# A two-layer decoder trunk on one core: the instruction planner's count of needed buffers, its look-ahead limits, the order of the mixers' steps, and an early preparation of one weight block

## The chip, the core and the metric

The program runs on 1 core of one Trainium2 chip. The metric is the device time of one execution in microseconds (us). One execution of the kernel before was recorded by the hardware profiler, and all rows in this text come from that recording. The engines are named as the profile names them: PE multiplies matrices, PEld loads its weights, DVE (VectorE) and ACT (ScalarE) work element by element, POOL is GpSimd, and SP only issues transfers.

## What is computed

A sequence of 512 positions with 1024 features goes through two layers. Each layer adds three normalized branches to x:

```python
for i in range(DEPTH):                       # DEPTH = 2
    h = rmsnorm(x, mix_pre_g[i])
    z = h @ w_in[i]                          # split into the inputs of three mixers
    out_a = spatial_gating(...)              # 4 groups of 64, chunks of 128 positions
    out_b = silu(r_g) * rms(retention(...))  # 6 heads of 64, a state carried over 4 chunks
    out_c = forgetting_attention(...)        # 6 heads of 64, softmax with decay
    x = x + rmsnorm(concat(out_a, out_b, out_c) @ w_o[i], mix_post_g[i])
    h = rmsnorm(x, ffn_pre_g[i])
    f = (gelu(causal_conv3(h @ w_gate[i])) * (h @ w_up[i])) @ w_down[i]   # width 4096
    x = x + rmsnorm(f, ffn_post_g[i])
    gate = sigmoid(rmsnorm(x, ple_pre_g[i]) @ w_ple_gate[i])
    x = x + rmsnorm((p[i] @ w_ple_proj[i]) * gate, ple_post_g[i])
```

## The kernel before

Products of full precision are made of three faster ones: `split` writes a high part (a cast on ACT) and a low part (a subtraction on DVE) of each operand, and `mm3` issues three matmuls (high with high, high with low, low with high). The positions are four chunks c of 128 (`NCH`), the 1024 features eight blocks of 128 (`KB`).

A layer is recorded by four functions in turn. `mixers` runs a list of steps: u and s the gating, F and v values of attention and retention, g0 to g2 and L the retention's gate (L is its Silu), f, a the projections and the softmax of a pair of attention heads, r, c those of a pair of retention heads. Each writes blocks of the concatenated result `cc`. `out_proj` multiplies `cc` by w_o: the first 512 columns (banks `wo0`) feature block by feature block in `O_ORDER` as the blocks of `cc` come, then the other 512 chunk by chunk. When a chunk is complete, `post_chunk` makes the row sums, the normalized branch (`fo`) and the new x, and `nxt` makes h, whose transposes (`hps`) PE computes. `ffn` works through 32 blocks b of 128 features. For the gate and up projections each block uses seven products instead of eight (12 matmuls of 128x256 each): the class `Seven` makes the seven sums of h that stand on their left (`hb..`, `hh..`, `hd`), and `gate_up` the sums of the weights that stand on their right. A block's weights come as `graw` (two transfers of 512 KB); from it come `wg` (split of the raw weights), `wu`, then four additions in place on `graw`, then `wsa` and `wsb` (splits of the sums). PE accumulates b11 and h6 in `beta`, b21 and d in `ag`, and ACT copies `beta` to `gs` after each of b11 and h6; the product h6 (`beta<-hh,wsa`) adds to the same place, so it follows the first copy. `down` multiplies the activations of four blocks by w_down (`dn`). `embed_operands` and the `eps` matmuls make p @ w_ple_proj for `ple`. All transfers are issued on SP's one queue.

Nothing of this is issued where it is written. A class `Plan` records every operation, and at the end `issue` simulates the engines with a cost for each operation and fixes the order of every engine's instructions; the chip then runs each engine's list in that order, with waits between engines. An operation whose inputs are ready is taken when it also has its buffers. The limits are:

- `AHEAD`: a buffer is not taken if its first use lies more than so many operations ahead of the oldest unfinished one; there is a number for each stage (`gu0` for the first four blocks of `ffn`, `gu` for the others, `emb`, `wo2` and so on).
- `live[tag]` counts, for every operation of the written order, how many buffers of a kind are needed there; a buffer is taken ahead of its turn only where that leaves enough. `inside[c]` is the same count for the two sets of 8 KB buffers (`SETS`: X has 18, W has 6; `wg`, `wsa` and `wsb` live only in W).

`SWITCH` is what the planner charges PE for going from one kind of matmul to another, and `warm` (in the changed code) stands for PE's full clock. All operations are issued from one line, L444 (L448 in the changed code), so the tile's name tells what an instruction is.

Of the kernel before, what the change touches and what calls it, by code (L numbers as in the profile page):

```python
# [50 lines left out]
class Plan:  # L51
# [153 lines left out]
    def cost(self, engine, method, outs, ins, args, kw):  # L205
# [13 lines left out]
        if engine == "PE":  # L219
            if method == "transpose":  # L220
                return 108, 0, n, "T"
            dt, rows = kw["lhsT"].dtype, kw["lhsT"].shape[0] / P
            if dt == F32R:
                return 0.4427 * n, 0, n * rows, n
            half = 0.5 if kw["lhsT"].shape[0] == 64 or kw["lhsT"].shape[-1] == 64 else 1
            return half * max(222, n * 4 / 2.4 + 4), 0, 2 * n * rows, "F"
        if engine == "ACT":
# [19 lines left out]
    def issue(self):  # L247
        ops = self.ops
        n = len(ops)
# [33 lines left out]
        order = []  # L283
        then, kind = None, "T"
        parked = {tag: [] for tag in (*slots, *(f"b8 {k}" for k in (*self.SETS, None)))}
# [65 lines left out]
        def complete(i, now):  # L351
            nonlocal front
            freed = []
            for t in set(ops[i][5]):
                uses[t] -= 1
                if not uses[t]:
                    tag = self.tiles[t][0]
                    heapq.heappush(slots[tag], now)
                    if t in self.kind:
                        c, k = self.place[t]  # L360
                        heapq.heappush(unused[c], (now, k))
                        freed += [f"b8 {k}" for k in (*self.SETS, None)]
                    freed.append(tag)
# [24 lines left out]
        while len(order) < n:  # L388
            progress = False
            for e in names:  # L390
# [3 lines left out]
                if ready[e] and free[e] <= now:  # L394
# [7 lines left out]
                    if e == "PE":  # L402
                        then = self.follows.get(i)
                        if ops[i][6][3] != kind:
                            busy += self.SWITCH.get(kind, 0) + (95 if ops[i][6][3] == "F" else 25 if ops[i][6][3] == 512 else 0)
# [112 lines left out]
def body(ctx, tc, a, out):  # L518
# [299 lines left out]

    def mixers(l, hT, uv):
        rs = hT.rs  # L820
# [243 lines left out]
        fq, rq = {}, {}  # L1064
        for step in "u F s g1 f0 g0 v a0 f1 a1 g2 r0 f2 L c0 r1 a2 r2 c1 c2".split():
            h = int(step[1]) if len(step) > 1 else 0
# [14 lines left out]
            elif step == "L":  # L1081
                A.activation(sg, sg, AF.Silu)
            elif step[0] == "f":
                fq[h] = fox_proj(h)
# [9 lines left out]

    def out_proj(l, cc, x, new, g, nxt):

# [20 lines left out]
        tm_chunk_major(cc, u, 512, done, O_ORDER, (0, 2, 1, 3))  # L1117
        return emb

    def ffn(l, hs, emb, x, new, g, nxt):  # L1120
        h = hs.t
# [15 lines left out]
        def gate_up(b, between):  # L1137
            raw = b8("graw", (2048,))
            load(raw, a["w_gu"][l, b].rearrange("p s n -> p (s n)"))
            u2, u1, g1, g2 = (raw[:, i * 512:i * 512 + 512] for i in range(4))  # L1140
            wg = b8("wg", (2, 1024), F32R)
            split(wg[:, 0, :], wg[:, 1, :], raw[:, 1024:2048])
            wu = [wk("wu", dt=F32R) for _ in range(2)]
            split(wu[0], wu[1], u2)
            for t, by in ((g1, u1), (u1, u2), (u2, g1), (g2, u2)):
                V.tensor_tensor(out=t, in0=t, in1=by, op=ALU.add)
            sa = b8("wsa", (2, 1024), F32R)
            split(sa[:, 0, :], sa[:, 1, :], raw[:, 0:1024])
            sb = b8("wsb", (2, 1024), F32R)
            split(sb[:, 0, :], sb[:, 1, :], raw[:, 1024:2048])  # L1150

            beta, ag = bank("beta"), bank("ag")
# [202 lines left out]
    for l in range(DEPTH):  # L1355
        cc = mixers(l, hT, uv)
        g = Gains(("mix_post_g", l), ("ffn_pre_g", l))
        hs = Seven(g)
        emb = out_proj(l, cc, Rows(src), xd[3 * l], g, hs)
        g = Gains(("ffn_post_g", l), ("ple_pre_g", l))  # L1360
        hT = Plain(g)
        ffn(l, hs, emb, Rows(xd[3 * l]), xd[3 * l + 1], g, hT)
        last = l + 1 == DEPTH
# [32 lines left out]
```

## Time and profile before

| | |
|---|---|
| median of 3 executions | 1589.41 us (1588.22 to 1592.01) |
| profiled execution | 1587.76 us, of it 1585.7 us in the span of the core |
| PE busy | 1559.8 us, 98% of the span |
| DVE busy | 1233.2 us, 78% |
| ACT busy | 837.2 us, 53% |
| POOL busy | 91.3 us, 6% |
| mean granted PE clock | 0.996 of full speed |

The span is the stretch from the first to the last instruction; the execution's own time holds 2.1 us more. Busy times of different engines overlap. In rows of instructions the columns are the start in us, the duration, engine and line, operation, output and inputs by the names in the program (buffer numbers left out), the tile's size, and how many instructions were joined; in brackets stands how long the engine stood idle before and which instruction of which engine ended that.

### The profile page before, as it was taken

The numbers are of one execution on the slowest core, as the hardware profiler recorded it, in microseconds if no ns is written. First come the engines' busy times: TensorE is split into PE (matmuls) and PEld (weight loads), VectorE is DVE, ScalarE is ACT, GpSimd is POOL, SyncE is SP. The second block draws the span as 40 slices with busy tenths as digits, with TensorE's granted clock in tenths as the row PEclk, the third lists the DMA queues.
The fourth block names the chain that finished last, engine by engine and source line by source line (L and its number), as shares of the span: only waits on it lengthen the run. The fifth ranks groups of instructions, "written<-read, shape, count | busy, mean of one in ns | idle before, by whom it ended". The sixth has DMA issues, their size and how long they took to land.

```text
span 1585.7 us, 25202 instructions
## 1 busy us (share of the span) xinstructions
PE 1559.8 (98%) x10034; PEld 1388.1 (88%) x10034; DVE 1233.2 (78%) x2013; ACT 837.2 (53%) x1380; POOL 91.3 (6%) x157
## 2 busy tenths in 40 slices
PE   7999998999999999999999999989999999999998
PEld 6887787999999999998888777889999999999987
DVE  6556869988878888878664658699887897898785
ACT  7324637665555555554552446477655555555453
POOL 1100020000000000002220000200000000000021
PEclk9999999999999999999999999999999999999999
DMA  8113147223323422424463023362332233234433
GB/s 316 68 55 107 61 168 265 81 80 115 125 81 103 137 80 88 153 100 180 179 250 107 28 80 116 125 252 81 108 116 97 92 123 106 83 131 134 148 141 124
DMA packets 63421, 197.47 MB, mean 125 GB/s; under 512 B 7348, under 2 KB 15164, under 8 KB 63304
## 3 DMA queue, kind: packets, MB, share of 16 engines
q1 hardware_dynamic: 63160, 195.81, 35.1%
q8 instruction: 78, 1.28, 0.3%
q14 instruction: 39, 0.32, 0.1%
q10 hardware_dynamic: 144, 0.07, 0.0%
HBM read 178.52 MB, written 17.33 MB: 124 GB/s over the span
## 4 chain that ended last, share of the span: by engine, by line
PE 95%; DVE 2%; DMA 1%; ACT 1%; POOL 0%; issue 0%; SPq 0%; POOLq 0%; DVEq 0%; ACTq 0%
PE beta L444 22%; PE dn L444 22%; PE ag L444 16%; PE ps L444 15%; PE rps L444 4%; PE fps L444 4%; PE gps L444 2%; PE wo L444 2%; PE sps L444 1%; PE hps L444 1%; PE tps L444 1%; PE ops L444 1%; PE rops L444 1%; DMA graw<-in_w_gu_dram 1%; PE ips L444 0%
## 5 line engine op out<-in xcount | busy, mean ns | idle before, releaser
L444 PE MATMUL dn<-thl,act 128*128 128x512 f32 x1536 | 371.4, 391 | 0.0
L444 PEld LDWEIGHTS dn<-thl,act 128*128 128x128 f32 x1536 | 279.9, 188 | 51.9
L444 PE MATMUL ps<-thl,hT 128*128 128x512 f32 (+3 forms) x984 | 207.1, 368 | 0.1
L444 PEld LDWEIGHTS ps<-thl,hT 128*128 128x128 f32 x984 | 177.0, 189 | 23.3 <-DVE thl L444 1.2
L444 DVE TENSOR_TENSOR graw<-graw 128x512 f32<-128x512 f32 x256 | 169.2, 684 | 1.0
L444 DVE TENSOR_TENSOR thl<-traw,thl 128x1024 fp32r<-128x1024 f32 (+2 forms) x120 | 140.4, 1184 | 13.6 <-ACT thl L444 13.6
L444 ACT CAST thl<-traw 128x1024 fp32r<-128x1024 f32 (+2 forms) x120 | 120.1, 1018 | 9.0 <-DMA traw<-in_w_pg_dram 4.6
L444 PE MATMUL beta<-hh,wsa 128*128 128x256 f32 x768 | 101.4, 281 | 7.8 <-ACT gs L444 7.5
L444 PEld LDWEIGHTS beta<-hh,wsa 128*128 128x128 f32 x768 | 94.7, 192 | 8.7 <-ACT gs L444 7.9
L444 PEld LDWEIGHTS beta<-hb,wg 128*128 128x128 f32 x768 | 97.7, 189 | 4.9
L444 PEld LDWEIGHTS beta<-hh,wu 128*128 128x128 f32 x768 | 98.2, 189 | 4.2
L444 PE MATMUL beta<-hh,wu 128*128 128x256 f32 x768 | 100.4, 280 | 0.0
L444 PE MATMUL beta<-hb,wg 128*128 128x256 f32 x768 | 99.9, 278 | 0.0
L444 PE MATMUL ag<-hb,wg 128*128 128x256 f32 x768 | 98.6, 276 | 0.0
L444 PE MATMUL ag<-hd,wsa 128*128 128x256 f32 x768 | 98.5, 278 | 0.0
L444 PE MATMUL beta<-hh,wsb 128*128 128x256 f32 x768 | 98.4, 276 | 0.0
L444 DVE SCALAR_TENSOR_TENSOR cv<-gs,cw,cv 128x511 f32<-128x511 f32 (+1 forms) x128 | 95.1, 743 | 3.6 <-ACT cv L444 3.5
L444 PE MATMUL ag<-hb,wsb 128*128 128x256 f32 x768 | 97.9, 276 | 0.0
L444 ACT ACTIVATE cv<-gs,cw 128x512 f32<-128x512 f32 x64 | 52.2, 816 | 82.4 <-DVE gs L444 82.4
L444 ACT COPY gs<-beta 128x256 f32<-128x256 f32 x128 | 47.2, 371 | 88.4 <-PE beta L444 86.6
L444 DVE TENSOR_TENSOR wsb<-graw,wsb 128x1024 fp32r<-128x1024 f32 x64 | 78.0, 1219 | 19.8 <-ACT wsb L444 15.0
L444 PEld LDWEIGHTS ag<-hd,wsa 128*128 128x128 f32 x768 | 93.1, 190 | 0.0
(193 smaller groups left out, 2655.7 us busy)
## 6 DMA issues: line engine op xcount, KB each, us to landing
graw<-in_w_gu_dram SPq DMA_DIRECT2D x128, 512.0 KB, 6.2
traw<-in_w_dn_dram SPq DMA_DIRECT2D x64, 512.0 KB, 5.0
x<-x SPq DMA_DIRECT2D x40, 512.0 KB, 5.0
fraw<-in_w_fm_dram SPq DMA_DIRECT2D x30, 512.0 KB, 8.8
traw<-in_w_wo_dram SPq DMA_DIRECT2D x16, 512.0 KB, 4.2
traw<-in_w_pg_dram SPq DMA_DIRECT2D x16, 512.0 KB, 8.6
x<-in_x_dram SPq DMA_DIRECT2D x8, 512.0 KB
traw<-in_w_uv_dram SPq DMA_DIRECT2D x8, 512.0 KB, 8.1
```

Of the source, the lines that this page charges most:

```text
L444: made = o[1](*[self.map(v) for v in o[2]], **{k: self.map(v) for k, v in o[3].items()})
```

## The change

Four edits stand beside each other. (1) When the last user of a buffer completes, `issue` now lowers `live` and `inside` from the oldest unfinished operation up to that buffer's last use, so that buffers that were taken and returned ahead of their turn are no longer counted as needed. (2) `AHEAD`, `SWITCH` and the clock's model have other numbers, and matmuls of 64 rows or columns are a kind of their own. (3) The mixers' steps and the last two of `O_ORDER` stand in another order. (4) The weight work of a block is a function of its own, `gate_up_weights`, and for block 0 it is recorded in `out_proj` after the first completed chunk (`EARLY`), in place of `gate_up`. The chip's instructions are the same in number and shape, but for ACT's table loads, 15 in place of 17.

```diff
-    AHEAD = {"mix": 460, "wo": 230, "wo2": 230, "emb": 185, "gu0": 720, "gu": 460, "dn": 245, "end": 770, "pg": 450, "pg2": 120}
+    AHEAD = {"mix": 595, "wo": 404, "wo2": 214, "emb": 291, "gu0": 1206, "gu": 523, "dn": 1028, "end": 1710, "pg": 555, "pg2": 142}
-    SWITCH = {"F": 110, "T": 9}
+    SWITCH = {"F": 40, "H": 310, "T": 9}
...
                     heapq.heappush(slots[tag], now)
+                    live[tag][front:last[t] + 1] -= 1
                     if t in self.kind:
                         c, k = self.place[t]
+                        inside[c][front:last[t] + 1] -= 1
                         heapq.heappush(unused[c], (now, k))
...
-                        if columns.get(now // self.TICK - 1, 0) < self.WARM:
+                        if not warm:
                             busy *= 2
-                        tick = (now + busy) // self.TICK
-                        columns[tick] = columns.get(tick, 0) + ops[i][6][2]
+                            tick = (now + busy) // self.TICK
+                            columns[tick] = columns.get(tick, 0) + ops[i][6][2]
+                            warm = columns.get(now // self.TICK - 1, 0) >= self.WARM
...
-O_ORDER = (0, 1, 5, 6, 7, 2, 3, 4)
+STEPS = "u g1 F g0 f0 s v f1 a0 g2 L a1 f2 r0 r1 a2 c0 r2 c2 c1"
+O_CHUNKS = (0, 2, 1, 3)
+EARLY = {0: 0}
+O_ORDER = (0, 1, 5, 6, 7, 2, 4, 3)
...
-        for step in "u F s g1 f0 g0 v a0 f1 a1 g2 r0 f2 L c0 r1 a2 r2 c1 c2".split():
+        for step in STEPS.split():
...
+    def gate_up_weights(l, b):
+
+        stage, plan.stage = plan.stage, "gu0" if b < 4 else "gu"
+        raw = b8("graw", (2048,))
+        load(raw, a["w_gu"][l, b].rearrange("p s n -> p (s n)"))
+        u2, u1, g1, g2 = (raw[:, i * 512:i * 512 + 512] for i in range(4))
+        wg = b8("wg", (2, 1024), F32R)
+        split(wg[:, 0, :], wg[:, 1, :], raw[:, 1024:2048])
+        wu = [wk("wu", dt=F32R) for _ in range(2)]
+        split(wu[0], wu[1], u2)
+        for t, by in ((g1, u1), (u1, u2), (u2, g1), (g2, u2)):
+            V.tensor_tensor(out=t, in0=t, in1=by, op=ALU.add)
+        sa = b8("wsa", (2, 1024), F32R)
+        split(sa[:, 0, :], sa[:, 1, :], raw[:, 0:1024])
+        sb = b8("wsb", (2, 1024), F32R)
+        split(sb[:, 0, :], sb[:, 1, :], raw[:, 1024:2048])
+        plan.stage = stage
+        return wg, wu, sa, sb
...
+            if len(seen) in EARLY:
+                ready[EARLY[len(seen)]] = gate_up_weights(l, EARLY[len(seen)])
+            seen.append(c)
...
+            wg, wu, sa, sb = gate_up_weights(l, b) if b not in ready else ready[b]
```

What this does to the issued order is seen in rows of the two orders. The first place is DVE at the entry of layer 0's `ffn`. Numbers tell tiles apart: before, `graw_1969` holds block 0's weights, and `graw_2352` those of block 1.

```order
L444 TENSOR_TENSOR graw_1969<-graw_1969 128x512
L444 TENSOR_TENSOR wg_2420<-graw_2352,wg_2420 128x1024
L444 TENSOR_TENSOR hh4_2290<-s4_2425,hh4_2290 128x4x128
L444 TENSOR_TENSOR graw_1969<-graw_1969 128x512
L444 TENSOR_TENSOR wu_2444<-graw_2352,wu_2414 128x512
L444 TENSOR_TENSOR graw_1969<-graw_1969 128x512
L444 TENSOR_TENSOR graw_2352<-graw_2352 128x512
L444 TENSOR_TENSOR graw_1969<-graw_1969 128x512
L444 TENSOR_TENSOR graw_2352<-graw_2352 128x512
L444 TENSOR_TENSOR wsa_2459<-graw_1969,wsa_2459 128x1024
L444 TENSOR_TENSOR gs_2474<-ag_2469,gs_2474 128x256
```
In the changed order block 0's weights are `graw_1913`, and its additions stand in `out_proj`, among the first chunks' `fo` and x.

```order
L448 TENSOR_TENSOR graw_1913<-graw_1913 128x512
L448 TENSOR_TENSOR fo_2092<-wo0_1713,gain_1903 128x512
L448 TENSOR_TENSOR fo_2092<-wo0_1761,gain_1903 128x512
L448 TENSOR_TENSOR graw_1913<-graw_1913 128x512
L448 TENSOR_TENSOR fo_2106<-wo0_1768,gain_1903 128x512
L448 TENSOR_TENSOR fo_2106<-wo0_1809,gain_1903 128x512
L448 TENSOR_TENSOR fo_2092<-ps_2049,gain_1903 128x512
L448 TENSOR_TENSOR graw_1913<-graw_1913 128x512
L448 SCALAR_TENSOR_TENSOR x_1874<-fo_2092,y_2113,x_1874 128x1024
L448 TENSOR_TENSOR graw_1913<-graw_1913 128x512
L448 TENSOR_TENSOR wsa_2130<-graw_1913,wsa_2130 128x1024
```
All four additions and `wsa` of block 0 stand now ahead of every h of `out_proj`. Before, they stood behind the last of the seven sums of h, alternating with the same work for block 1.

The second place is ACT just ahead of the first copy of `beta` to `gs`, before the change.

```order
L444 CAST hh7_2266<-s7_2400 128x4x128
L444 CAST hh6_2258<-s6_2405 128x4x128
L444 CAST wu_2414<-graw_2352 128x512
L444 COPY e_2322<-eps_2396 128x512
L444 CAST wg_2420<-graw_2352 128x1024
L444 CAST hh4_2290<-s4_2425 128x4x128
L444 COPY e_2354<-eps_2422 128x512
L444 CAST wu_2437<-graw_2375 128x512
L444 COPY e_2354<-eps_2440 128x512
L444 CAST wsa_2459<-graw_1969 128x1024
L444 COPY gs_2474<-beta_2450 128x256
```
The cast of `wsa` for block 0 stands directly ahead of the copy. In the changed order there are two pieces; in the first, the casts of block 0's `wu`, `wg` and `wsa` stand behind `pT`, the transposed p of `embed_operands`.

```order
L448 CAST pT_2051<-pps_2041 128x256
L448 CAST pT_2051<-pps_2046 128x256
L448 CAST wu_2060<-graw_1913 128x512
L448 CAST wg_2068<-graw_1913 128x1024
L448 CAST pT_2051<-pps_2063 128x256
L448 ACTIVATE junk_100,s1_2102<-ps_2049 128x512
L448 CAST wsa_2130<-graw_1913 128x1024
```
The second piece is the one that ends in the same copy.

```order
L448 CAST wg_2403<-graw_2258 128x1024
L448 COPY e_2312<-eps_2381 128x512
L448 CAST wg_2421<-graw_2275 128x1024
L448 COPY s22_2433<-hps_2419 128x512
L448 COPY e_2383<-eps_2401 128x512
L448 CAST hd_2266<-sd_2430 128x4x128
L448 CAST hb22_2288<-s22_2433 128x4x128
L448 CAST hh6_2282<-s6_2442 128x4x128
L448 COPY e_2383<-eps_2428 128x512
L448 CAST hh7_2273<-s7_2460 128x4x128
L448 COPY gs_2482<-beta_2445 128x256
```
In place of the cast of block 0's `wsa` there stand two `wg` of the blocks 1 and 2 (`graw_2258`, `graw_2275`), farther ahead. On SP the loads of the blocks 1 to 3 follow those of x in one piece now, ahead of the first stores of e.

The third place is PE from the transposes of the first chunks' h up to h6 of block 0, before the change.

```order
L444 MATMUL hps<-k_ident,h 128x128 x4
L444 MATMUL eps<-ehl,pT 128x512 x3
L444 MATMUL hps<-k_ident,h 128x128 x4
L444 MATMUL eps<-ehl,pT 128x512 x18
L444 MATMUL hps<-k_ident,h 128x128 x8
L444 MATMUL eps<-ehl,pT 128x512 x18
L444 MATMUL beta<-hb_2163,wg 128x256 x12
L444 MATMUL ag<-hb_2175,wg 128x256 x12
L444 MATMUL beta<-hh_2258,wsa 128x256 x2
L444 MATMUL beta<-hb_2163,wg 128x256 x5
L444 MATMUL beta<-hh_2258,wsa 128x256 x10
```
In the changed order the same stretch reads as follows.

```order
L448 MATMUL hps<-k_ident,h 128x128 x4
L448 MATMUL eps<-ehl,pT 128x512
L448 MATMUL hps<-k_ident,h 128x128 x4
L448 MATMUL eps<-ehl,pT 128x512 x24
L448 MATMUL hps<-k_ident,h 128x128 x4
L448 MATMUL eps<-ehl,pT 128x512
L448 MATMUL hps<-k_ident,h 128x128 x4
L448 MATMUL eps<-ehl,pT 128x512 x7
L448 MATMUL beta<-hb_2179,wg 128x256 x12
L448 MATMUL ag<-hb_2191,wg 128x256 x12
L448 MATMUL beta<-hb_2179,wg 128x256 x3
L448 MATMUL beta<-hh_2282,wsa 128x256 x12
```
More `eps` stand between the second and the third group of transposes, fewer behind the fourth, and three matmuls of block 1 stand ahead of h6 (`beta<-hh_2282,wsa`).

## Rows read from the trace of the kernel before

**Rows 1.** The page: busy time by engine, and the chain that ended last.

```profile
PE 1559.8 (98%) x10034; PEld 1388.1 (88%) x10034; DVE 1233.2 (78%) x2013; ACT 837.2 (53%) x1380; POOL 91.3 (6%) x157
...
PE 95%; DVE 2%; DMA 1%; ACT 1%; POOL 0%; issue 0%; SPq 0%; POOLq 0%; DVEq 0%; ACTq 0%
```
**Rows 2.** Waits of PE: for what, us in total, times, longest us.

```profile
PE hps L444 <- DVE h L444: 7.9, 1, 7.9
PE beta L444 <- ACT gs L444: 7.5, 2, 3.8
PE hps L444 <- ACT wg L444: 1.8, 2, 0.9
PE cps L444 <- DVE ro L444: 1.2, 2, 0.7
PE beta L444 <- DVE wsa L444: 0.3, 1, 0.3
```
**Rows 3.** Timeline of PE, entry of layer 0's `ffn`.

```profile
254.72 4.36 PE L444 MATMUL eps<-ehl,pT 128*128 128x512 f32 x18
...
260.33 1.58 PE L444 MATMUL ag<-hb,wg 128*128 128x256 f32 x12
265.68 0.51 PE L444 MATMUL beta<-hh,wsa 128*128 128x256 f32 x2 [3.77 <-ACT gs L444]
```
**Rows 4.** Timeline of PE, the same place in layer 1.

```profile
1049.28 0.80 PE L444 MATMUL beta<-hh,wsa 128*128 128x256 f32 x2 [3.75 <-ACT gs L444]
```
**Rows 5.** Timeline of ACT, the same place in layer 0.

```profile
264.31 1.04 ACT L444 CAST wsa<-graw 128x1024 fp32r<-128x1024 f32 x1 [1.71 <-DVE graw L444]
265.26 0.36 ACT L444 COPY gs<-beta 128x256 f32<-128x256 f32 x1
```
**Rows 6.** Timeline of DVE, the same place in layer 0.

```profile
252.77 1.41 DVE L444 SCALAR_TENSOR_TENSOR h<-x,rs,gain 128x512 f32<-128x512 f32 x2 [1.44 <-POOL rs L444]
...
263.59 2.49 DVE L444 TENSOR_TENSOR graw<-graw 128x512 f32<-128x512 f32 x4
266.00 1.22 DVE L444 TENSOR_TENSOR wsa<-graw,wsa 128x1024 fp32r<-128x1024 f32 x1
```
**Rows 7.** Timeline of SP, block 1's weights in layer 0.

```profile
251.44 1.43 SPq L444 DMA_DIRECT2D graw<-in_w_gu_dram  x2
```
**Rows 8.** Windows: length, busy us of PE, PEld, DVE, ACT, POOL, PE clock, DMA share, GB/s.

```profile
220.00:240.00 20.00, 20.00 (x98) 16.49 (x97) 13.78 (x22) 10.54 (x27) 4.84 (x14) 1.00 0.13 53
...
266.00:270.00 4.00, 3.71 (x20) 3.41 (x19) 4.00 (x7) 2.23 (x4) 0.00 (x0) 0.57 1.04 420
...
1049.00:1055.00 6.00, 5.72 (x26) 5.70 (x27) 6.00 (x9) 3.01 (x5) 0.00 (x0) 0.51 1.04 416
...
311.00:671.00 360.00, 360.00 (x2581) 336.74 (x2581) 302.94 (x431) 194.10 (x297) 0.00 (x0) 1.00 0.31 106
```
**Rows 9.** Timeline of PE in the mixers: two kinds of matmul in turn.

```profile
121.84 0.48 PE L444 MATMUL gps<-hT,fhl 128*128 128x512 f32 x1
122.16 0.38 PE L444 MATMUL tps<-k_ident,pe 128*128 128x128 f32 x2
```
**Rows 10.** Timeline of ACT in the mixers: the Silu of step L.

```profile
128.79 1.28 ACT L444 ACT_TABLE_LOAD   x1
130.08 1.49 ACT L444 ACTIVATE mix<-mix 128x1536 f32<-128x1536 f32 x1
```
**Rows 11.** Timeline of PE, then of ACT, in the steady part of `ffn`.

```profile
411.36 0.84 PE L444 MATMUL beta<-hh,wsa 128*128 128x256 f32 x6
...
410.20 0.37 ACT L444 COPY gs<-beta 128x256 f32<-128x256 f32 x1
```
**Rows 12.** Timeline of POOL (two places), then of DVE at the second place.

```profile
161.72 0.25 POOL L444 TENSOR_SCALAR vh<-ss 128x8 f32<-128x8 f32 x1 [38.31 <-DVE ss L444]
...
202.22 1.14 POOL L444 TENSOR_SCALAR vh<-ss 128x8 f32<-128x8 f32 x1 [38.48 <-DVE ss L444]
...
202.05 1.22 DVE L444 TENSOR_TENSOR thl<-traw,thl 128x1024 fp32r<-128x1024 f32 x1
```

More of the change, by code (lines that the diff above doesn't have):

```diff
@@ L224, in cost @@
                 return 0.4427 * n, 0, n * rows, n
-            half = 0.5 if kw["lhsT"].shape[0] == 64 or kw["lhsT"].shape[-1] == 64 else 1
-            return half * max(222, n * 4 / 2.4 + 4), 0, 2 * n * rows, "F"
+            if kw["lhsT"].shape[0] == 64 or kw["lhsT"].shape[-1] == 64:
+                return 0.5 * (n * 4 / 2.4 + 4), 0, 2 * n * rows, "H"
+            return max(222, n * 4 / 2.4 + 4), 0, 2 * n * rows, "F"
         if engine == "ACT":
@@ L283, in issue @@
         order = []
-        then, kind = None, "T"
+        then, kind, warm = None, "T", False
         parked = {tag: [] for tag in (*slots, *(f"b8 {k}" for k in (*self.SETS, None)))}
@@ L404, in issue @@
                         if ops[i][6][3] != kind:
-                            busy += self.SWITCH.get(kind, 0) + (95 if ops[i][6][3] == "F" else 25 if ops[i][6][3] == 512 else 0)
+                            busy += self.SWITCH.get(kind, 0) + {"H": 95, 512: 25}.get(ops[i][6][3], 0)
                             kind = ops[i][6][3]
                     if e == "PE":
-                        if columns.get(now // self.TICK - 1, 0) < self.WARM:
+                        if not warm:
                             busy *= 2
-                        tick = (now + busy) // self.TICK
-                        columns[tick] = columns.get(tick, 0) + ops[i][6][2]
+                            tick = (now + busy) // self.TICK
+                            columns[tick] = columns.get(tick, 0) + ops[i][6][2]
+                            warm = columns.get(now // self.TICK - 1, 0) >= self.WARM
                     if self.table.get(i) not in (None, table):
@@ L816, in body, with mixers @@
     cums = [[dram(f"cums{l}_{h}", (1, S)) for h in range(6)] for l in range(DEPTH)]
-    def mixers(l, hT, uv):
+    def mixers(l, hT, uv, ready):
         rs = hT.rs
@@ L1082, in mixers @@
                 A.activation(sg, sg, AF.Silu)
+            elif step[0] == "p":
+                ready[h] = gate_up_weights(l, h)
             elif step[0] == "f":
@@ L1093, in mixers, with out_proj @@
         return cc
-    def out_proj(l, cc, x, new, g, nxt):
+    def gate_up_weights(l, b):
[15 more added lines that the diff above has]
+        return wg, wu, sa, sb
+    def out_proj(l, cc, ready, x, new, g, nxt):
         plan.stage = "wo"
@@ L1116, in done, with ffn @@
             nxt(c, x[c])
-        tm_chunk_major(cc, u, 512, done, O_ORDER, (0, 2, 1, 3))
+            if len(seen) in EARLY:
+                ready[EARLY[len(seen)]] = gate_up_weights(l, EARLY[len(seen)])
+            seen.append(c)
+        seen = []
+        tm_chunk_major(cc, u, 512, done, O_ORDER, O_CHUNKS)
         return emb
-    def ffn(l, hs, emb, x, new, g, nxt):
+    def ffn(l, hs, emb, ready, x, new, g, nxt):
         h = hs.t
@@ L1137, in gate_up @@
         def gate_up(b, between):
[L1138 to L1150, printed above, removed]
+            wg, wu, sa, sb = gate_up_weights(l, b) if b not in ready else ready[b]
             beta, ag = bank("beta"), bank("ag")
@@ L1355, in body @@
     for l in range(DEPTH):
-        cc = mixers(l, hT, uv)
+        ready = {}
+        cc = mixers(l, hT, uv, ready)
         g = Gains(("mix_post_g", l), ("ffn_pre_g", l))
         hs = Seven(g)
-        emb = out_proj(l, cc, Rows(src), xd[3 * l], g, hs)
+        emb = out_proj(l, cc, ready, Rows(src), xd[3 * l], g, hs)
         g = Gains(("ffn_post_g", l), ("ple_pre_g", l))
         hT = Plain(g)
-        ffn(l, hs, emb, Rows(xd[3 * l]), xd[3 * l + 1], g, hT)
+        ffn(l, hs, emb, ready, Rows(xd[3 * l]), xd[3 * l + 1], g, hT)
         last = l + 1 == DEPTH
```

## The prediction, made before the changed kernel ran

> **What bounds the kernel now.** I read the page first. PE is busy for 1559.8 of 1585.7 us, and the chain that ended last runs over PE for 95% [rows 1]. The matmuls are the same in number and shape after the change, so it can take from the time only what PE spends idle, at a lower clock, or on going from one kind of matmul to another. The second view was therefore PE's list of waits [rows 2]. It holds five lines, 18.7 us in sum. The largest, 7.9 us, is the program's start (the first h must exist before PE transposes it), which no edit touches. The others are two stalls of 3.8 us on ACT's `gs`, two of 0.9 us in front of transposes of h (`hps`), two of about 0.6 us on `ro`, and one of 0.3 us on `wsa`.
>
> The third view was PE's timeline at these stalls. Both long ones lie at the same place, the entry of `ffn`: in layer 0 PE reaches h6 of block 0 (`beta<-hh,wsa`) and stands idle for 3.77 us [rows 3], in layer 1 for 3.75 us [rows 4]. The reader should see in ACT's rows why [rows 5]: the copy `gs`, which needs only the product b11, stands in ACT's list right behind the cast of block 0's `wsa`. That cast waited 1.71 us for DVE's additions on `graw`, and DVE came to them late: four in a row began at 263.59 us and took 2.49 us, and the second half of `wsa` followed at 266.00 [rows 6]. So PE waited for the weights of block 0, by way of a copy that had nothing to do with them but its place in a queue.
>
> The fourth view was the windows around the stalls [rows 8]. The granted clock is 1.00 in the steady part and in a window ahead of the stall, but 0.57 over the 4 us behind the first stall and 0.51 over the 6 us behind the second: the lower of PE's two levels (1.2 in place of 2.4 GHz) for most of each. It fell after PE had stood idle.
>
> **The change, part by part.** *Early weights of block 0.* The orders show its load, both casts, the four additions and `wsa` ahead of every h of `out_proj`. DVE has room there: it is busy 13.78 of 20 us in 220:240, while PE is busy for all of the 20 [rows 8]. What is moved is one split of 1024 columns (1.22 us on DVE [rows 6]) for each of `wg` and `wsa`, half of one for `wu`, and four additions at 2.49/4 = 0.62 us each, so some 5.5 us of DVE work for 6.2 us of room in that window alone. Cover gone, it would delay the chunks' x by what doesn't fit. With the cast out of the way, `gs` follows b11. Behind b11 PE has b21 (12 matmuls of 128x256, 1.58 us [rows 3]) and now three matmuls of block 1, 0.13 us each by the same row, 0.4 us. So the copy of 0.36 us [rows 5] has some 1.5 us to begin in. Ahead of it on ACT stand a cast and a copy of 512 columns. Following ACT and DVE through the new order by hand with durations of the trace, I find h6 ready 0.3 to 0.6 us before PE comes to it, in either layer. Removed: 7.5 us for `gs`, and 0.3 us for the wait on `wsa`.
>
> *The clock.* If PE doesn't stand idle there, it doesn't fall. The windows give the loss: (1 - 0.57) x 4.00 + (1 - 0.51) x 6.00 = 1.7 + 2.9 = 4.6 us; the 0.3 us wait lies inside, so 4.3 us are taken. Lower bound nothing, if the clock falls all the same.
>
> *Waits for transposes.* The profile names ACT's `wg` for 1.8 us, but DVE's row shows what was late: h waited 1.44 us for POOL's rs [rows 6]. Between the second and third group of transposes there are 24 `eps` now, 18 before; six more at 4.36/18 = 0.24 us [rows 3] are 1.5 us of cover. By hand all four groups come 0.35 to 0.9 us early. Removed: 1.8 us.
>
> *Waits on `ro`.* They stay: 1.2 us [rows 2]. The last two heads' outputs are computed back to back now and meet the same chain over ACT, POOL and DVE.
>
> *The mixers' steps.* Counted in the two orders, PE's stretches of the fast kind of matmul between others go from 137 to 130. A 512-column matmul alone between transposes takes 0.32 us from start to start [rows 9], against 0.24 in a run; by this 7 x 0.08 = 0.6 us are saved. The other kinds cost more to leave, as far as the rows of narrow matmuls let one tell, so I put 1.4 above and take 1.0 us. Two table loads of 1.28 us [rows 10] go too, but on ACT and off the path. Step L stands between two softmaxes now: load, Silu and load again, 1.28 + 1.49 + 1.28 = 4.05 us on ACT [rows 10], while PE has projections to do.
>
> *New waits.* A new order of this length will have some that no row of before shows. Below: nothing. Above: half of the old stall at one place in each layer, 3.8 us. The nearest rows are the tight places that do wait now, 0.6 us each on `ro`; two of that size make 1.2, and I take 1.0 us.
>
> *The count of needed buffers and `AHEAD`* cost nothing by themselves. They let SP load the blocks 1 to 3 earlier: before, block 1's load was issued at 251.44 us [rows 7]; in the new order its place is some 44 matmuls sooner, about 10 us. These loads pass e's stores, for which nothing waits before `ple`.
>
> The sum is made against the profiled execution of 1587.76 us, 1.65 us under the median: -7.5 - 0.3 - 4.3 - 1.8 - 1.0 + 1.0 = -13.9 us, so 1573.9, and with 1.65 put back **1575.5 us**. With the bounds of steps and new waits the sum goes from -15.3 to -10.7, so 1574.1 to 1578.7; a `ro` wait that vanishes, and the 1.2 us by which the fastest shown run lies under the median, put the low end at 1572.
>
> **Rivals.** *B, part of the gain is given back at the transposes (1578 to 1583 us).* Between x and h of a chunk, where DVE stood idle for POOL's rs, it now runs `wsb`, two `hb` and `wu`: 1.22 + 3 x 0.61 = 3.1 us (the split of [rows 6], and half of it for each of the three of 512 columns). A small POOL operation, 0.25 us when DVE is quiet, took 1.14 us when a split ran beside it [rows 12]. The Trainium skill, page "SBUF — State Buffer", says that DVE and GpSimd share a port pair that one of them holds alone for a whole instruction, a DVE operation with two inputs in SBUF against a GpSimd one that reads SBUF among them. The row agrees: 0.89 us more, ending just behind the split. By the row, rs's two operations cost up to 1.8 us more, and DVE comes to h up to 3.1 - 1.4 = 1.7 us later; less the cover of 1.5 us this is up to 2.0 us a layer, 4.0 us. That gives 1575.5 - 1.0 + 4.0 = 1578.5. If the clock falls there too, all 4.3 us of it come back: 1582.8. Against it: the two delays overlap rather than add, and the clock fell before only behind idle stretches of 3.75 us and more [rows 3, 4].
>
> *C, the stall stays (1587 to 1591).* On ACT two casts `wg` of the blocks 1 and 2, about 1.04 us each as the row of `wsa` [rows 5], stand ahead of `gs` now; they wait for loads. If these land late, by a few us, `gs` is held in the same way, and with the clock all 12.1 us are back: 1587.6. For it: in the window behind the first stall the transfers are at a share of 1.04 and 420 GB/s [rows 8], full. Against it: the loads are issued earlier by 10 us, and their buffers are free by then.
>
> *S, slower: the steady part.* In it `gs` ends at 410.20 + 0.37 = 410.57 us and its reader begins at 411.36 [rows 11], 0.79 us of margin. DVE is busy there 303 of 360 us [rows 8], so little slack is left for a new order. A cast of 1.04 us that gets ahead of `gs` overruns the margin by 0.25 us. In all 64 blocks that is 16 us, 1591.5, no change; a copy of 0.37 us more makes 0.62 us a block, 40 us, 1615. It decides for slower from (13.9 + 3.2)/64 = 0.27 us a block. Against it: PE's order in the steady part is the same, and ACT is busy only 194 of 360 us.
>
> **How the numbers follow.** A measurement of this kernel tells about 0.2% from no change, 3.2 us. The forecast has 0.62 (1572 to 1578.7), B 0.21, C 0.09, S 0.08, of which 0.06 end slower. Faster is the forecast and B, 0.83; the same is C and the mild S, 0.11; slower 0.06. The range of 8 in 10 is the forecast's and B's: 1571.5 to 1584.
>
> **What would show it.** Right: PE's list of waits holds no `gs`, `wg` or `wsa`, `hps` only at the start, the clock is 1.00 through the entry of both `ffn`, and ACT's `wsa` lies some 20 us ahead of h6. For B, a wait of `hps` on DVE's h, and POOL's rows around it longer than when undisturbed. For C, `gs` behind a `wg` that a transfer ended. For S, more than 360 us for the same stretch of products. The prediction is wrong if new waits in the mixers, which I followed least exactly, pass 4 us, or if the clock falls at a place where it held.

## The result, and the profile after

The changed kernel takes 1580.01 us (median of 4 executions, 1579.35 to 1581.86), the kernel before 1588.99 us (4 executions). The ratio is 0.9942, with a 95% interval of 0.9925 to 0.9959: 9.0 us faster. The forecast was 1575.5 us, in a range of 1571.5 to 1584. The profiled execution took 1579.35 us with a span of 1577.6 us, against 1585.7 us before. PE's busy time is 1559.8 us in both.

PE's list of waits first, to be read against [rows 2]: for what, us in total, times, longest.

```profile
PE hps L448 <- DVE h L448: 9.0, 4, 7.9
PE tps L448 <- DVE pe L448: 0.8, 2, 0.4
PE cps L448 <- DVE ro L448: 0.4, 2, 0.2
```
The lines on `gs`, `wg` and `wsa` are gone, 9.6 us. The wait on `ro` is 0.4 us in place of 1.2. New are 1.1 us on h (the rest of its line is the program's start) and 0.8 us on `pe`, the softmax's result. The list is 8.5 us shorter. The entry of `ffn` on PE's timeline, in layer 0 and then in layer 1:

```profile
259.85 1.58 PE L448 MATMUL beta<-hb,wg 128*128 128x256 f32 x12
261.26 1.58 PE L448 MATMUL ag<-hb,wg 128*128 128x256 f32 x12
262.68 0.52 PE L448 MATMUL beta<-hb,wg 128*128 128x256 f32 x3
263.03 1.58 PE L448 MATMUL beta<-hh,wsa 128*128 128x256 f32 x12
...
1039.21 1.53 PE L448 MATMUL beta<-hb,wg 128*128 128x256 f32 x12
1040.58 1.52 PE L448 MATMUL ag<-hb,wg 128*128 128x256 f32 x12
...
1042.28 1.52 PE L448 MATMUL beta<-hh,wsa 128*128 128x256 f32 x12
```
PE goes from b11 to h6 without a stop in both layers, where it stood for 3.8 us before [rows 3, 4]. ACT's rows show what moved: `wsa` of block 0 is cast at 231 us, 31 us ahead of the first copy to `gs`.

```profile
230.99 1.05 ACT L448 CAST wsa<-graw 128x1024 fp32r<-128x1024 f32 x1 [2.35 <-DVE graw L448]
...
262.33 0.37 ACT L448 COPY gs<-beta 128x256 f32<-128x256 f32 x1
```
The windows behind the old stalls and in the steady part, with columns as in [rows 8]:

```profile
220.00:240.00 20.00, 19.91 (x97) 16.24 (x95) 15.64 (x23) 11.40 (x27) 4.31 (x12) 1.00 0.13 53
...
266.00:270.00 4.00, 4.00 (x37) 4.00 (x36) 4.00 (x7) 3.41 (x5) 0.00 (x0) 1.00 1.03 417
...
1049.00:1055.00 6.00, 6.00 (x56) 6.00 (x55) 6.00 (x10) 5.18 (x8) 0.00 (x0) 1.00 1.03 422
...
311.00:671.00 360.00, 360.00 (x2587) 336.99 (x2587) 303.01 (x432) 195.03 (x297) 0.00 (x0) 1.00 0.32 109
```
The clock is 1.00 where it was 0.57 and 0.51. In the steady part PE is busy for all of the 360 us, as before. DVE does 15.64 us of work in 220:240, 13.78 before: the early weights fill room that was there.

### The profile page after: what moved, and what is told of

Read it like the earlier page. It is cut to its first block, busy times and chain, and to the rows that moved or that the text cites. A ratio compares the mean times of both kernels' runs of the same rounds, so it can differ in the third digit from the quotient of the medians.

```text
span 1577.6 us, 25214 instructions
## 1 busy us (share of the span) xinstructions
PE 1559.8 (99%) x10034; PEld 1389.4 (88%) x10034; DVE 1229.2 (78%) x2013; ACT 838.2 (53%) x1378; POOL 92.8 (6%) x157
## 4 chain that ended last, share of the span: by engine, by line
PE 94%; DVE 3%; ACT 1%; DMA 1%; issue 1%; POOL 0%; SPq 0%; POOLq 0%; DVEq 0%; ACTq 0%
PE beta L448 22%; PE dn L448 22%; PE ag L448 17%; PE ps L448 15%; PE fps L448 4%; PE rps L448 3%; PE wo L448 3%; PE gps L448 2%; PE hps L448 1%; PE sps L448 1%; PE eps L448 1%; PE tps L448 1%; ACT rr L448 1%; DVE rm L448 1%; PE rops L448 1%; PE ops L448 1%
## 5 line engine op out<-in xcount | busy, mean ns | idle before, releaser
L448 ACT CAST thl<-traw 128x1024 fp32r<-128x1024 f32 (+2 forms) x120 | 120.6, 1022 | 36.2 <-DVE wsb L448 18.9
L448 PE MATMUL beta<-hh,wsa 128*128 128x256 f32 x768 | 97.8, 277 | 0.0
L448 ACT ACTIVATE cv<-cv 128x512 f32<-128x512 f32 x64 | 40.5, 632 | 107.4 <-DVE cv L448 107.4
L448 PEld LDWEIGHTS ag<-hb,wg 128*128 128x128 f32 x768 | 92.8, 188 | 0.3
L448 PEld LDWEIGHTS beta<-hh,wsb 128*128 128x128 f32 x768 | 92.1, 188 | 0.4 <-ACT gs L448 0.4
```

The source lines that it names most:

```text
L448: made = o[1](*[self.map(v) for v in o[2]], **{k: self.map(v) for k, v in o[3].items()})
```

## The experiments

All times are medians, ratios are to executions of the kernel before from the same set of runs (1588.7 to 1589.2 us). Kernels built from the changed one are called by what was put back, those built from the kernel before by what was added.

| edits in the kernel | median us | ratio, 95% interval |
|---|---|---|
| all (the changed kernel) | 1580.0 | 0.9942 (0.9925 to 0.9959) |
| early weights alone | 1594.2 | 1.0030 (1.0018 to 1.0043) |
| order of steps alone | 1630.8 | 1.0260 (1.0246 to 1.0274) |
| count alone | 1593.6 | 1.0027 (1.0017 to 1.0036) |
| count and early weights | 1589.0 | 0.9996 (0.9987 to 1.0004) |
| count and order of steps | 1627.8 | 1.0244 (1.0230 to 1.0258) |
| all but the early weights | 1593.4 | 1.0026 (1.0017 to 1.0034) |
| all but the order of steps | 1592.4 | 1.0024 (1.0015 to 1.0033) |
| all but the count | 1631.8 | 1.0269 (1.0255 to 1.0283) |
| all but the look-ahead limits | 1608.4 | 1.0122 (1.0108 to 1.0135) |
| all but the planner's costs | 1587.1 | 0.9984 (0.9975 to 0.9993) |
| all, and three short matmuls more | 1579.6 (one execution) | none |

### Which edit makes the gain

The first four kernels set theory 1, that the early weights alone free `gs` and make the gain, against two rivals: the count and the look-ahead, or the order of the steps.

**Early weights alone**, the kernel before with this:

```diff
+EARLY = {0: 0}
+            if len(seen) in EARLY:
+                ready[EARLY[len(seen)]] = gate_up_weights(l, EARLY[len(seen)])
+            seen.append(c)
```

> The kernel before (1589.0 us) with the early weights of block 0 alone: old count of buffers, old look-ahead, old planner costs, old order of the mixers' steps. Theory 1 (the gain of 9 us comes from taking the cast of block 0's wsa out of ACT's list ahead of gs, and the early recording alone does that): the two waits on gs (7.5 us) and the two stretches at the lower clock (4.3 us) are gone, 1577 to 1580 us. Theory 2 (the count of buffers and the look-ahead make it, the early recording only goes along): little changes, 1586 to 1590 us. Theory 3 (the order of the mixers' steps makes it): 1588 to 1590 us.

All three theories missed: 1594.2 us, slower than before. The waits on `gs` and `wsa` are gone, but the line on h has grown from 7.9 to 18.3 us:

```profile
PE hps L444 <- DVE h L444: 18.3, 6, 7.8
```
The place is the last chunk's transposes, in both layers (4.77 and 4.79 us). PE's rows in layer 0:

```profile
250.04 1.64 PE L444 MATMUL eps<-ehl,pT 128*128 128x512 f32 x6
256.45 1.97 PE L444 MATMUL hps<-k_ident,h 128*128 128x128 f32 x8 [4.77 <-DVE h L444]
```
Most of the cause is in PE's own list. Between the second and the third group of transposes stand 6 `eps` here, 18 before and 24 in the changed kernel; the other 30 stand behind the fourth group. Against the kernel before, the 12 fewer are 2.7 us less cover (1.64 us in place of 4.35). The same stretch in the changed kernel:

```profile
251.38 5.72 PE L448 MATMUL eps<-ehl,pT 128*128 128x512 f32 x24
```
The other part is that h comes later: it begins 5.6 us behind the start of that stretch of `eps`, and 4.4 us behind it in the kernel before. DVE shows why:

```profile
249.31 1.22 DVE L444 TENSOR_TENSOR wsb<-graw,wsb 128x1024 fp32r<-128x1024 f32 x1
250.45 1.28 DVE L444 SCALAR_TENSOR_TENSOR x<-fo,y,x 128x1024 f32<-128x1024 f32 x1
...
255.65 1.41 DVE L444 SCALAR_TENSOR_TENSOR h<-x,rs,gain 128x512 f32<-128x512 f32 x2
```
`wsb`, 1.22 us, stands ahead of x there, and h comes 5.2 us behind that x. Between them ACT takes the sum of squares of x late, at 253.36 us, since casts and copies of other transposes stand ahead of it in its list:

```profile
253.36 1.06 ACT L444 ACTIVATE junk<-x 128x1024 bf16<-128x1024 f32 x1
```
Of the 3.9 us that this wait is longer than before (4.8 in place of 0.9), 2.7 us are thus the missing `eps` and 1.2 us the later h. It is the place of the forecast's rival B, at two and a half times its price (10.4 us of wait in place of 4.0), but not by B's mechanism. The clock falls there too, to the lower level for 6.8 us in each layer (0.50 from 254.3 and from 1042.8 us). In the changed kernel `wsb` stands behind x, and DVE's row for h keeps only 0.46 us of idle time; h comes 4.7 us behind x, only 0.5 us sooner than above, but with 24 `eps` ahead of its transposes PE doesn't wait for it in layer 0:

```profile
251.53 1.29 DVE L448 SCALAR_TENSOR_TENSOR x<-fo,y,x 128x1024 f32<-128x1024 f32 x1
252.72 1.23 DVE L448 TENSOR_TENSOR wsb<-graw,wsb 128x1024 fp32r<-128x1024 f32 x1
...
255.06 0.69 DVE L448 TENSOR_TENSOR wu<-graw,wu 128x512 fp32r<-128x512 f32 x1
256.21 1.42 DVE L448 SCALAR_TENSOR_TENSOR h<-x,rs,gain 128x512 f32<-128x512 f32 x2 [0.46 <-POOL rs L448]
```
**All but the early weights:**

```diff
-EARLY = {0: 0}
+EARLY = {}
```

> The changed kernel (1580.0 us) without the early weights of block 0. Theory 1: the stall comes back at the entry of both layers; in the issued order gs stands behind two casts of block 0 now, wsa and wsb, so 3.8 to 5 us of wait on gs in each layer and the lower clock behind it: 1590 to 1594 us. Theory 2: 1579 to 1582 us. Theory 3: 1579 to 1582 us.

The time was as theory 1 had it, 1593.4 us, but the place was not. PE goes through the entry and stops two blocks later, at 292 to 307 us (and at 1079 to 1094 us in layer 1), for `wsa` and `gs` of DVE:

```profile
292.00 1.43 PE L448 MATMUL beta<-hh,wsa 128*128 128x256 f32 x10 [0.53 <-DVE wsa L448]
...
304.39 1.43 PE L448 MATMUL beta<-hh,wsa 128*128 128x256 f32 x10 [1.61 <-DVE wsa L448]
307.06 2.93 PE L448 MATMUL ag<-hd,wsa 128*128 128x256 f32 x12 [1.25 <-DVE gs L448]
```
**Order of steps alone**, `STEPS` and `O_ORDER` of the change in the kernel before:

```diff
-        for step in "u F s g1 f0 g0 v a0 f1 a1 g2 r0 f2 L c0 r1 a2 r2 c1 c2".split():
+        for step in "u g1 F g0 f0 s v f1 a0 g2 L a1 f2 r0 r1 a2 c0 r2 c2 c1".split():
...
-O_ORDER = (0, 1, 5, 6, 7, 2, 3, 4)
+O_ORDER = (0, 1, 5, 6, 7, 2, 4, 3)
```

> The kernel before with the new order of the mixers' steps and the new order of the concatenated blocks alone. Theory 1: both stalls on gs stay, and the two parts ahead of the entry, which together took 0.9 us more in the changed kernel than before, take 0 to 2 us more here too: 1588 to 1591 us. Theory 3: 1579 to 1583 us.

Both ranges missed, by 40 and 48 us. PE waits in the mixers, and at the entry for `gs` as before:

```profile
PE tps L444 <- DVE pe L444: 15.3, 11, 2.4
PE hps L444 <- DVE h L444: 12.2, 6, 7.8
PE beta L444 <- ACT gs L444: 6.4, 2, 5.2
```
PE's idle time is 25.5 us more than before. The clock adds to it: the record has it at the lower level for 37 us, in six places of the mixers and of the entries, where the kernel before has 10 us.

**All but the order of steps**, the same edit the other way round in the changed kernel.

> The changed kernel with the old order of the mixers' steps and of the concatenated blocks, all else as changed. Theory 1: no wait on gs, the clock stays; the mixers are free to be 0 to 2 us quicker in each layer than in the changed kernel: 1577 to 1581 us. Theory 3: the gain is gone, 1586 to 1590 us.

1592.4 us, so theory 1's number failed here too. There is no wait on `gs` at the entry and no fall of the clock; the time goes elsewhere. From the first matmul to the first of b11 it takes 2.6 us more than the changed kernel, and `ffn` of layer 0 takes 3.2 us more (in layer 1 it is 2.5 and 4.0 us), with a wait that comes back with every fourth block (305.89, 366.58 and 427.49 us are the first three):

```profile
PE ag L448 <- DVE gs L448: 4.3, 12, 0.4
```
So theory 1 fell, and its two rivals with it: no single edit is the gain. Theory 2's pair, the count and the look-ahead, fell as part of a kernel without the early weights; alone it wasn't run. The next three kernels ask which parts of the planner the others need.

**All but the count:**

```diff
-                    live[tag][front:last[t] + 1] -= 1
...
-                        inside[c][front:last[t] + 1] -= 1
```

> The changed kernel (1580.0 us) without the edit of the count: buffers that came back ahead of their turn are still counted as needed. In its issued order the last chunk's transposes follow the first ones with no eps between, so h of the last chunk has little cover. Theory 4 (the count is what lets the early weights in without pushing the last chunks' h back): 3 to 5 us of wait on h in each layer with the lower clock behind it, 1588 to 1594 us. Theory 5 (the planner's costs for PE, not the count, make the mixers' new order work, and look-ahead and count matter little): 1578 to 1583 us.

The side was theory 4's, the size far past it: 1631.8 us. The three longest waits follow; in all PE is idle for 32.6 us more than in the changed kernel, and the clock is at the lower level for 41 us, in six places.

```profile
PE hps L446 <- DVE h L446: 17.7, 5, 7.7
PE beta L446 <- ACT gs L446: 9.0, 7, 3.5
PE tps L446 <- DVE pe L446: 7.9, 8, 2.2
```
**All but the look-ahead limits**, `AHEAD` as before.

> The changed kernel with the old look-ahead limits. Theory 4: the entry of ffn stays free of the wait on gs, since the early weights are recorded ahead and the count leaves them their buffers: 1578 to 1585 us. Rival (the wider limits for the first four blocks and for p @ w_ple_proj, 1206 and 291, are what lets the weights of the blocks 1 to 3 and the eps fill the entry): waits on h, wsa or gs of 3 us and more in each layer, 1586 to 1592 us.

The rival was nearer, but 1608.4 us is past both. The waits have moved into the retention (`rm`, its masked products) and back to h. They are not all of it: behind the two on `rm` and at the entry of both `ffn`, where PE waits for `hb` (the high part of a sum of h), the clock stands at the lower level for 31 us in four places:

```profile
PE hps L448 <- DVE h L448: 10.5, 5, 7.7
PE ips L448 <- DVE rm L448: 8.2, 2, 4.1
```
**All but the planner's costs**, with `SWITCH`, the kinds and the clock's model as before (the model's numbers are the same in both kernels; in the changed one the clock rises once and never falls).

> The changed kernel with the planner's old costs for PE: the old charges for a change of kind, no kind of their own for matmuls of 64 rows or columns, the old model of the clock. Its issued order at the entry of ffn is that of the changed kernel. Theory 5: the mixers' new order is placed badly, as it was with the order of steps alone (15 us of waits on pe, the softmax's result), and 10 to 40 us are lost: 1590 to 1620 us. Theory 4: 1578 to 1583 us.

1587.1 us, between the two theories: 7 of the 9 us are gone, without the collapse that theory 5 had. Waits on `ro` (2.7 us) and on `pT` (the transposed p, 2.6 us) make 5.3 us.

The last three kernels try theory 6, that no edit brings the gain alone and the count only lets the planner place what the others move. **Count alone** (the diff of the count above, added to the kernel before):

> The kernel before (1589.0 us) with the edit of the count alone. In its issued order the copy gs stands behind the casts of block 0's wsa and wsb, and more eps stand ahead of the last chunks' transposes. Theory 6 (no edit brings the gain alone; the count only lets the planner place what the others move): the stall moves from gs to wsa and the entry is no quicker, 1586 to 1592 us. Rival (the count is the gain, the rest is decoration): 1579 to 1583 us.

1593.6 us: the rival fell, and theory 6's range was missed by 1.6 us. The stall didn't move to `wsa` either; PE now waits for `gs` of ACT and of DVE, in many short stops. The clock doesn't fall anywhere before the end, and all idle stretches of PE together are 18.1 us, 18.9 before. So idle time doesn't explain the loss; two other things show in PE's rows. Ahead of b11 it takes 1.6 us more than before in layer 0 and 2.6 us in layer 1, with 0.5 us more of idle time in the two: the stretches of the fast kind of matmul between others are 12 more than before, where the changed kernel has 7 fewer. That these changes of kind are the cost is likely, not shown. And in `ffn` a stop costs more than its idle time: PE is idle for 0.71 us ahead of a matmul at 294.50 us, and this matmul begins 0.99 us behind the one ahead of it, the next one another 0.22 us later, where 0.113 us is usual; so 0.27 us are lost beside the idle time. The two `ffn` have 16 stops, which makes some 4 us (an estimate from this one).

**Count and early weights:**

> The kernel before with the edit of the count and the early weights of block 0; old order of the mixers' steps, old look-ahead, old costs. With the early weights alone the last chunk's transposes came 4.8 us late in each layer and the time was 1594 us. Theory 6: with the count the planner finds other work to put there, the wait on h falls under 1.5 us a layer, gs is free as well: 1578 to 1585 us. Rival (the early weights crowd DVE and ACT whatever the count): a wait of 3 us and more on h in each layer, 1590 to 1596 us.

1589.0 us, the same as before and above theory 6's range. What theory 6 said of the waits held (1.4 us on h beside the start's, 0.7 on ACT's `gs`), and the clock holds through both entries, but the pair didn't bring the time. 36 `eps` and 8 transposes in each layer have moved behind the first matmul of b11; with some 9.5 us put back for them (36 of 0.24 and 8 of 0.11 us), the stretch ahead of b11 takes some 3 us more than before in each layer, 0.5 to 0.7 us of it idle time, and `ffn` some 3 us less. The stretches of the fast kind are 10 more than before here, as with the count alone. So the entry's saving is spent in the mixers.

**Count and order of steps:**

> The kernel before with the edit of the count and the new order of the mixers' steps; no early weights, old look-ahead, old costs. The order of steps alone took 1631 us, with 15 us of waits on the softmax's pe and clock falls in the mixers. If the count is what makes that order possible, those waits are under 3 us and the time is 1587 to 1595 us. If the look-ahead of the mixers (595 in place of 460) is needed for it too, most of the loss stays: 1610 to 1632 us.

1627.8 us: the look-ahead, not the count alone, is needed for that order. The clock is at the lower level for 34 us, and the longest waits are now on the retention's state and result:

```profile
PE cps L446 <- DVE ro L446: 5.7, 2, 3.3
PE tps L446 <- DVE pe L446: 5.1, 8, 1.2
PE rops L446 <- DVE R L446: 5.0, 2, 3.6
```
### What the cadence of matmuls costs

In the changed kernel's rows above, 12 matmuls of 256 columns take 1.41 us from start to start in layer 0 (259.85 to 261.26) and 1.37 us in layer 1 (1039.21 to 1040.58), at a granted clock of 1.00: 118 and 114 ns each. **Three short matmuls more**, in layer 0 only:

```diff
+            if self.stages[i] == "gu0" and o[0] == "PE" and kw.get("start") and self.half < 3 and o[2][0].shape[-1] == 256 and o[2][0].offset == 256:
+                self.half += 1
+                made = o[1](self.map(o[2][0][:, 0:128]), **{**kw, "rhs": kw["rhs"][:, 0:128], "stop": False})
```

> The changed kernel with three matmuls more in layer 0: ahead of the product d of the blocks 0, 1 and 2 its first matmul is issued once over only 128 of the 256 columns, and overwritten by the whole one. This is for the cadence: in the changed kernel the matmuls of 256 columns follow each other every 118 ns from 259.9 to 297.9 us and every 113 ns from then on, with the clock granted in full. If the two cadences are two stable ways in which a weight load stands to the matmul ahead of it, a short one throws PE from one into the other, and the stretch at 118 ns ends at one of the three places (265, 275, 284 us): some 0.8 to 1.4 us less up to block 4. If the cadence comes from the tiles or from what the other engines or transfers do, it stays at 118 ns to 297 us, and the three cost some 0.2 us.

PE's rows around the three:

```profile
262.86 1.52 PE L454 MATMUL beta<-hh,wsa 128*128 128x256 f32 x12
...
264.68 0.22 PE L451 MATMUL ag<-hd,wsa 128*128 128x128 f32 x1
...
266.20 1.58 PE L454 MATMUL beta<-hh,wsb 128*128 128x256 f32 x12
...
274.56 0.22 PE L451 MATMUL ag<-hd,wsa 128*128 128x128 f32 x1
...
276.06 1.52 PE L454 MATMUL beta<-hh,wsb 128*128 128x256 f32 x12
...
284.11 0.22 PE L451 MATMUL ag<-hd,wsa 128*128 128x128 f32 x1
...
285.63 1.58 PE L454 MATMUL beta<-hh,wsb 128*128 128x256 f32 x12
```
Durations tell it: 1.52 us for 12 at the quick cadence, 1.58 at the slow one. The stretch began quick this time, the first short matmul (264.68) threw it into the slow cadence, the second (274.56) back into the quick one, the third (284.11) into the slow one again. Behind the three, 82, 78 and 114 matmuls in a row keep the cadence that they were thrown into, with up to five uneven ones at each switch. So the first view was right, with a start that I had not foreseen, so that its 0.8 to 1.4 us could not be tested: two cadences, both stable, and a disturbance takes PE from one to the other. How a weight load stands to its matmul in either, no row shows. The same list of instructions began quick here and slow in the changed kernel's profile, so the tiles don't decide it.

## Why the prediction was right, and where it was not

From its own base the sum went 13.9 us down, the measurement 9.0 us. 1580.0 us lies in the range, but not in the forecast's own 1572 to 1578.7: it lies where rival B would have put it (1578 to 1583), and B did not decide. The mechanism at h6 was right; that the shortfall stayed within the range is luck in part. Where it lies, PE's starts show: the first matmul and the first of b11 of each layer before, and the first matmul of the changed kernel, whose b11 rows stand above.

```profile
7.89 1.97 PE L444 MATMUL hps<-k_ident,h 128*128 128x128 f32 x8 [7.89 <-DVE h L444]
...
258.91 1.58 PE L444 MATMUL beta<-hb,wg 128*128 128x256 f32 x12
...
1042.53 1.58 PE L444 MATMUL beta<-hb,wg 128*128 128x256 f32 x12
```
```profile
7.85 1.97 PE L448 MATMUL hps<-k_ident,h 128*128 128x128 f32 x8 [7.85 <-DVE h L448]
```
From the first matmul to b11 of layer 0 it is 251.02 us before and 252.00 after (+1.0), from there to b11 of layer 1 783.62 and 779.36 (-4.3), and on to the end of the span 543.2 and 538.4 (-4.8). The sum had put -12.1 us on the two entries of `ffn` and -1.8 us on what stands ahead of them. By its steps:

**The stall at h6, the clock, and the waits on `wsa` and `wg`** are gone as said, -7.5, -4.3 (the forecast's estimate; the clock is 1.00 there now), -0.3 and -1.8 us; the lists and windows above show each. The copy `gs` ends 0.33 us ahead of h6 in layer 0 (262.70 and 263.03) and 0.23 us in layer 1; by hand h6 was to be ready 0.3 to 0.6 us early.

**New waits** were put at 1.0 us. They are 1.9 us (1.1 on h, 0.8 on `pe`), inside the bounds. Those on `ro`, left standing, lost 0.8 us. Three waits on h beside the start's, where a right forecast was to show none, are one sign that failed: 0.41 us in `out_proj` of either layer (242.16 and 1021.18 us) and 0.33 us at the third group of transposes in layer 1 (1036.44 us). By hand all four groups were early.

**Rivals C and S** did not come. The two casts `wg` ahead of `gs` began without a wait (256.20 and 257.66 us); block 1's load was issued at 244.40 us, 7 us sooner than before, where 10 were forecast. PE is as busy in the steady part as before.

**Rival B** did not decide (its place shows in the 0.33 us of layer 1), but its pieces are there. POOL's rs took 0.57 us for one chunk and 0.87 us for the last:

```profile
239.80 0.57 POOL L448 TENSOR_TENSOR rs<-vh,minus_half 128x1 f32<-128x1 f32 x1
...
255.31 0.87 POOL L448 TENSOR_TENSOR rs<-vh,minus_half 128x1 f32<-128x1 f32 x1
```
That is 0.3 us more, where the forecast's row had 0.9 [rows 12]. DVE ran `wu` at that time (0.69 us from 255.06, in DVE's rows above), a shorter operation than the split there. By the Trainium skill, page "SBUF — State Buffer", section "SBUF: two separate sides", a DVE operation with two inputs in SBUF and a GpSimd one that reads SBUF don't share their port pair: the one that starts first has it for its whole instruction. The row agrees with it, but one row doesn't prove it: rs began 0.25 us into `wu` and ended 0.43 us behind it. Elsewhere rs took up to 0.99 us (at 245.92 us, beside DVE's sums of h).

**The mixers' steps** are the term that failed: I took 1.0 us off for fewer changes of kind. Ahead of b11 layer 0 takes 1.0 us more, with less idle time; it should have been shorter. The start makes 1.0 us of it: the clock rose later in this execution. The first matmuls of the kernel before, and then of the changed one:

```profile
9.95 6.26 PE L444 MATMUL ps<-thl,hT 128*128 128x512 f32 x17
16.05 0.60 PE L444 MATMUL hps<-k_ident,h 128*128 128x128 f32 x4
```
```profile
9.85 7.05 PE L448 MATMUL ps<-thl,hT 128*128 128x512 f32 x16
16.74 0.60 PE L448 MATMUL hps<-k_ident,h 128*128 128x128 f32 x4
```
16 matmuls of 512 columns took 6.89 us from start to start in the changed kernel, 17 took 6.10 us before, so with one more at 0.23 us it is 1.0 us more. It belongs to the execution, not the change: in the recorded clock of the profiles the rise comes anywhere from 13.3 to 16.1 us, and in the kernel with all but the early weights, whose list begins as the changed kernel's, it comes at 13.3 us in place of 16.0. With the start taken out, and with every idle stretch of PE counted, also those too short for the list of waits (1.55 us before and 1.31 after in this part, 1.68 and 1.58 in the mixers of layer 1), the matmuls themselves took some 0.2 us more in layer 0 and the same time in layer 1 (from the last `dn` of layer 0 to b11, 293.88 us in place of 293.96). The fewer changes of kind saved nothing that shows: some +0.2 us in place of -1.0.

**The cadence** is the cost that no term held. In the profiled executions 1214 of the 5376 matmuls of the gate and up products have the next one 116 to 121 ns behind them, before 795; most of the others 113 ns. 419 more at 4.6 ns are 1.9 us. The largest stretch is the one at the entry of layer 0, where before the stall ended it. This too varies between executions: with the three short matmuls it is 774 in layer 1, where the list is the changed kernel's, in place of 474.

The sum of what was found: idle time -8.1 (all stretches; 8.5 by the list), clock -4.3, start +1.0, mixers +0.2, cadence +1.9 make -9.3 us; the spans differ by -8.1. The 1.2 us left over are not settled.

**The planner's edits** were said to cost nothing by themselves. That sentence holds the misunderstanding. The count earns nothing by itself either (1593.6 us; look-ahead and costs were not run alone), yet without it the same early weights and steps cost 51.8 us more than with it, and without the look-ahead 28.4. The prediction treated the cast's place in ACT's list as the cause. For the stall that holds: with the early weights alone it is gone too. But a shortage of DVE may show there too. From 260 to 320 us DVE is busy for 59.0 of 60 us before, 59.4 in the changed kernel and 59.5 with the count alone. What differs is the work on weights that DVE has done by the first matmul of b11: 1.9 us before and 5.0 us with the count alone or without the early weights, and PE is idle for 3 to 5 us in `ffn` of layer 0; 9.6 us in the changed kernel and 10.2 with the early weights alone, and it is idle for 0.0 and 1.0 us. In these five it goes together, which proves no more: with the old steps DVE has done 12.2 us and PE is idle for 2.3, and without the count it is 7.0 and 6.7. Work done ahead isn't enough either: the early weights alone free the entry and lose the time at the transposes ahead of it. The sum came into the range because it was made from the issued order of the whole change, not from its parts.

Open stays which buffers bind the mixers' new order when count or look-ahead are old, and what the other pairs of edits would do; no run took that apart.

## What to carry to other kernels

Where a planner fixes the order, judge an edit by the order that comes out of all edits together: here four of five single reversals cost more than the whole gain, and each of the three additions tried alone made the kernel slower. A copy that waited behind someone else's work marked an engine with a full list behind it. Before moving the work, look in the windows for where that engine has room, and then at what the new order does on every other queue: here 6 `eps` in place of 24 between two groups of transposes went with a wait of 4.8 us, in a kernel whose stall was gone. Count lost clock with the wait ahead of it: two stalls of 3.8 us cost 11.8 us together with it (4.3 us of it by the windows). And count stops as well as idle time: a short one cost 0.27 us more than the list of waits shows.

## What the runs showed of the hardware

Matmuls of 128x256 have two stable cadences at a granted clock of 1.00, 113 and 118 ns from start to start. A single short matmul switched from one to the other, in either direction, in all three places tried. At 298 us, in both kernels, a weight load that began some 65 ns behind the matmul ahead of it, where 3 to 4 ns are usual in that stretch, ended the slow one. What makes the two is not known from these runs.

PE's clock at the program's start rose between 13.3 and 16.1 us after it, in executions of kernels whose first matmuls come at 7.6 to 7.9 us. In the middle it fell at idle stretches of PE: at the two of 3.8 us before, and at those of 4.8 us with the early weights alone (0.50 from 254.3 us). With all but the early weights it fell behind stops of 1.6 and 1.3 us that lie 2.7 us apart (lower level from 306.8 us), and with all but the planner's costs behind one of 1.9 us (from 226.8 us). It held at 0.4 us in the changed kernel and at stops of up to 1.3 us with the count alone.

Behind a stop PE lost more than the idle time: some 0.17 us until the first matmul and 0.11 us until the next, at a granted clock of 1.00 (0.71 us of idle time with the count alone, at 294.50 us).
